# Hybrid decoder block on one core: other places in the SBUF partition for the matmul operands

## The chip, the cores and the metric

One NeuronCore of a Trainium2 chip runs the whole program. The metric is the device time of one execution in microseconds (us); a run's number is that of the core. "Span" is the time from the first to the last instruction in a profiled execution.

## The reference

One decoder block on x of shape (1, 256, 2048) in float32, with a conditioning vector c:

```
mod = silu(c) @ w_ada + b_ada                      # six vectors of 2048: sh1, sc1, gt1, sh2, sc2, gt2
h = rms_norm(x, norm1_gain) * (1 + sc1) + sh1
p = h @ w_in + b_in                                # 2048 -> 8736 columns
y_rwkv = rwkv7_branch(p[...])                      # 16 heads of 64, a scan over the 256 tokens
y_attn = sliding_window_sink_attention(p[...])     # 16 heads of 64, window 128
merged = sig(g_rwkv) * (y_rwkv @ w_branch_rwkv) + sig(g_attn) * (y_attn @ w_branch_attn)
x = x + gt1 * (merged @ w_out)
h = rms_norm(x, norm2_gain) * (1 + sc2) + sh2
x = x + gt2 * (square(relu(h @ w_up)) @ w_down)    # 2048 -> 8192 -> 2048
return rms_norm(x, final_gain)
```

## The kernel before

**Matmuls in two halves.** Every big product runs in float32r with both operands split: a value is the sum of a rounded part "hi" and a rest "lo", and three of the four products are kept (hi·hi, hi·lo, lo·hi). A piece of 512 KB of weights is loaded into a tile `raw` (L286, L325, queue of SP); ScalarE casts it into `whi` (L274) and VectorE subtracts to get `wlo` (L275). There are 7 `raw`, 4 `whi` and 4 `wlo` buffers of 4096 bytes a partition. Every matmul record in the trace has a weight load (LDWEIGHTS, "PEld") of its stationary operand beside it.

**Two forms of product.** `feed` (L278) has the weights stationary (128 columns, 512 bytes a partition) and activations as the moving rows (256 tokens, 1024 bytes). One piece of weights makes 24 such matmuls:

```
for wt, xs in ((hi, (xh, xl)), (lo, (xh,))):            # L291
    for kk in range(n):
        ...
            for xx in xs:
                TE.matmul(ps[...], lhsT=wt[:, kk, o:o + m], rhs=xx(k), ...)   # L297
```

`rows_product` (L309) has it the other way round: 128 tokens of the activations are stationary and 512 columns of a weight part move (L319).

**Order of the work.** The four parts of the input product (L948 to L984, pieces of w_in over 4 blocks of k each, 384 matmuls in a part) come first, with the vectors sc1 and sh1 of the next part made beside them on VectorE by `ada_dve` (L207). Then come gates, keys and the attention branch's product with `a1` and `a2` as moving rows (L1006 to L1034), while the RWKV chain, attention and further `ada` vectors are put between the pieces by `pulse` (L253), in an order that is fixed when the program is built. Then: the RWKV branch's product with two `tt` tiles as moving rows (L1039), the output product (L1095, stationary rows `m`), the first three column products of the up matrix from rows not yet normalised (`zhi`, `zlo`, 258 columns, 96 matmuls in each product, L1111 to L1140), and the MLP in 8 groups: `up(g + 1)` (4 column products of 96 matmuls, rows `h2`), then `down(g)` (192 matmuls of 512 columns, stationary rows `u`, L1181). `ada_vec(5)` runs beside the MLP; its sums are small matmuls (L186) between the pieces.

**Places in the partition.** Pools stand one behind the other: `const`, `wp` (`raw`, `acc`, `whi`, `wlo`), `hp` (the four tiles of 8192 bytes that hold `h`, then `m`, then `h2`), and `mx`, which is closed after the branch products and whose room the pool `ml` takes. The address of a tile is the sum of the sizes before it, each rounded up to 32 bytes. Tag `ug` has three slots, each as long as its longest tile, 16512 bytes for `zlo`. From the sizes, in bytes from the start of the partition, and the rest by 512:

| tile | role in the matmul | place before | rest by 512 |
|---|---|---|---|
| whi, wlo | weights' parts | 56384 + 4096 i | 64 |
| h, m, h2 (hp) | moving, stationary, moving | 89152 + 8192 i | 64 |
| tt (two) | moving | 146496, 154688 | 64 |
| a1, a2 | moving | 186880, 195072 | 0 |
| zhi, zlo | moving, rows of 1032 bytes | 187840, 171328 | 448, 320 |
| u, slot 1 (groups 1, 4, 7) | stationary | 138304 | 64 |
| u, slot 2 (groups 0, 3, 6) | stationary | 154816 | 192 |
| u, slot 3 (groups 2, 5) | stationary | 171328 | 320 |

"Offset" below is the moving row's place less the stationary row's, as a rest by 512. Before the change it is 0 for `h`, `h2`, `tt` and `m`, 448 for `a1` and `a2`, and 0, 384 and 256 for `u` in slots 1, 2 and 3.

Of the kernel before, what the change touches and what calls it, by code (L numbers as in the profile page):

```python
# [10 lines left out]
F32 = mybir.dt.float32  # L11
F32R = mybir.dt.float32r
# [6 lines left out]
P = 128  # L19
T = 256  # L20
D = 2048
KC = D // P
# [16 lines left out]
RATE_BG = (0.9, 0.3, 0.4, 0.2)  # L39
RATE_Z = 2.0  # L40
NCH = T // L
NORM_EPS = 1e-6
GN_EPS = 64e-5
KAPPA = -math.exp(-0.5)
# [9 lines left out]
def _constants():  # L54
# [19 lines left out]
    k[:, K_DI + P:K_DI + 2 * P] = np.where((dp >= 0) & (dp < WIN), dp, far)  # L74
    rs = np.ones((NCH, L + 1), np.float32)
    rs[:, 0] = 0
    k[:, K_RS:K_RS + NCH * (L + 1)] = rs.reshape(1, -1)
    k[:, K_ON:K_ON + P] = 1.0
# [4 lines left out]
def hybrid_block(ctx: ExitStack, tc, x, c, w_ada, b_ada, norm1_gain, w_in, b_in, rwkv_mix, rwkv_w0,  # L83
# [4 lines left out]
    V, S, G, TE = nc.vector, nc.scalar, nc.gpsimd, nc.tensor  # L88

    const = ctx.enter_context(tc.tile_pool(name="const", bufs=1))  # L90
    wp = ctx.enter_context(tc.tile_pool(name="wp", bufs=2))
    hp = ctx.enter_context(tc.tile_pool(name="hp", bufs=1))
    mm = ctx.enter_context(tc.tile_pool(name="mm", bufs=NMM, space=PSUM))
    ax = ctx.enter_context(tc.tile_pool(name="ax", bufs=8 - NMM, space=PSUM))

# [9 lines left out]
    def ps_ax():  # L105
        return ax.tile([P, 512], F32, tag="ax", name=nm("ax"))
# [25 lines left out]
    mx = mx_ctx.enter_context(tc.tile_pool(name="mx", bufs=1, reuse_waits="tile"))  # L132

    def tl(tag, shape=(T,), bufs=1, dt=F32):
        return mx.tile([P] + list(shape), dt, tag=tag, bufs=bufs, name=nm(tag))
# [167 lines left out]
    def cols_product(w, kblocks, c0, widths, xh, xl):  # L303
        ps = ps_mm()
        for k0 in range(0, kblocks, 8):
            feed(w, k0, 8, [(c0, sum(widths))], [(ps, j, m) for j, m in enumerate(widths)], xh, xl, 0, kblocks - 1)
        return ps
# [61 lines left out]
    def rstd_of(dst, ss, n, eps, t):  # L369
        V.tensor_scalar(ss, ss, 1.0 / n, eps, op0=ALU.mult, op1=ALU.add)  # L370
        rsqrt(dst, ss, t)
# [20 lines left out]
    for tb in range(2):  # L392
        S.activation(sq, xt[tb][:], AF.Square, accum_out=st_s[:, tb:tb + 1])
    rstd_of(st_s[:, 2:4], st_s[:, 0:2], D, NORM_EPS, st_s[:, 4:6])
    for _ in range(2):
# [3 lines left out]
    for k2 in range(KC // 2):  # L399
        ps = ps_ax()  # L400
# [50 lines left out]
    def c4(t):  # L451
        return t.rearrange("p (c t) -> p c t", c=NCH)

# [26 lines left out]
    def prep(ss, st):  # L480
# [3 lines left out]
        g4 = st["g4"][:, j]  # L484
        st["ar"] = ar = tl("ar", (2, NCH, 2, L), 2)
        st["tok"] = tok = {n: tl(n, (2, NCH, L), 2) for n in ("vt", "bt", "kt")}
        st["bv"] = bv = tl("bv", (2, T), 2)
        for i in range(2):
            b = 2 * ss + i
            kT, rT, vT = [st["in"][:, n, i, :] for n in range(3)]  # L490
            p4 = tl("p4", (4 * T + NCH,), 2)
            aT, eN, kk = [p4[:, o * T:(o + 1) * T] for o in range(3)]
# [304 lines left out]


    W3 = 3 * P
    vtok = mx.tile([P, 2, P], F32, name="vtok")  # L800
    yad = tc.dram_tile([8, P, T], F32, name="yad")

    arena = [tl("a1", (8 * T,)), tl("a2", (8 * T,))]
# [1 line left out]
    def slot(a, o, n, shape):  # L805
        return arena[a][:, o:o + n].rearrange("p (a b) -> p a b", a=shape)
# [64 lines left out]
    def pair(q2, qT=None):  # L871
        if qT is None:
            qT = qas[q2 % 2]
            nc.sync.dma_start(qT.rearrange("p a b -> p (a b)"), qd[q2])
        yield from zipped([attention(2 * q2 + i, qT[:, i]) for i in range(2)])
# [19 lines left out]
    def begin_attention():  # L895
        kvf = slot(0, 0, 2 * T, 2)
        for i in range(2):
            S.activation(kvf[:, i, :], e_kv[:, i * T:(i + 1) * T], AF.Identity,
                         bias=colA[:, A_BK + i:A_BK + i + 1], scale=1.0)
        q0 = qas[0]  # L900
        for i in range(2):
            S.activation(q0[:, i, :], e_q[:, i * T:(i + 1) * T], AF.Identity, bias=q8[:, i:i + 1], scale=0.125)
        for kv in range(2):
            for hh in range(2):
                G.tensor_copy(kd[HS[hh], kv, :], kvf[HS[kv], 0, :])
        ps = ps_ax()
        for kb in range(2):
            TE.transpose(ps[:, kb * P:(kb + 1) * P], kvf[:, 1, kb * P:(kb + 1) * P], ident)
        S.copy(vtok[:].rearrange("p a b -> p (a b)"), ps[:, 0:2 * P])
        for q2 in range(4):  # L910
            att.append(pair(q2, q0 if q2 == 0 else None))

# [35 lines left out]
    for part, nk in enumerate(SL):  # L948
# [9 lines left out]
        for g2 in range(0, len(sums), 2):  # L958
            two = sums[g2:g2 + 2]
            ps = [ps_ax() for _ in two]  # L960
            feed(w_in, k0, nk, [(c, 256) for _, c in two], [(p, j, P) for p in ps for j in range(2)],
                 hA, hB, k0, k0 + nk - 1)
            for a, ((what, n), _) in enumerate(two):
                t, j = rest[g2 + a]
                o = flat(t, j)
                if part == 0:
                    S.copy(o, ps[a][:])
                else:
                    V.tensor_tensor(o, ps[a][:], o, op=ALU.add)  # L969
                if last:  # L970
                    t = t[:, 2 * j:2 * j + 2, :]
                    if what == "g":
                        gate_out(n, t, o)
                    elif what == "q":
                        for j in range(2):
                            S.activation(t[:, j, :], t[:, j, :], AF.Identity, bias=q8[:, 2 * n + j:2 * n + j + 1],
                                         scale=0.125)
                        nc.sync.dma_start(qd[n], o)
            if last and g2 == 2:
                finish(bg)  # L980
                begin_heads()
                begin_attention()
                rate["rw"], rate["att"] = RATE_RW, RATE_ATT
# [43 lines left out]
    for g in range(8):  # L1027
# [4 lines left out]
        ps = cols_product(w_branch_attn, 8, g * 256, [P, P], yh, yl)  # L1032
# [6 lines left out]
    for g in range(8):  # L1039
# [4 lines left out]
        ps = cols_product(w_branch_rwkv, 8, g * 256, [P, P], yh, yl)  # L1044
# [8 lines left out]


    ml = ctx.enter_context(tc.tile_pool(name="ml", bufs=1, reuse_waits="tile"))
    x1 = ml.tile([P, 2, D], F32, name="x1")
    for tb in range(2):
        nc.sync.dma_start(x1[:, tb, :], x[tb * P:(tb + 1) * P, :])
# [1 line left out]

    TW = T + 2
    zhi = ml.tile([P, KC, TW], F32R, tag="acc", name="zhi")
    zlo = ml.tile([P, KC, TW], F32R, tag="ug", bufs=3, name="zlo")
    wide = ml.tile([P, KC, P], F32, tag="fg", name="wide1")
    gt1 = ml.tile([P, D], F32, tag="gt", name="gt1")

    V.tensor_scalar(gtc[:, 0:KC], gtc[:, 0:KC], 0.5, None, op0=ALU.mult)
    ss2 = ml.tile([P, 16], F32, name="ss2")

    def scaled(ks):  # L1070
        for k in ks:
# [5 lines left out]
    def turned(cg):  # L1077
        for k in (cg * 4, cg * 4 + 2):
            ps = ps_ax()
            for i in range(2):  # L1080
                for tb in range(2):
                    TE.transpose(ps[:, i * T + tb * P:i * T + (tb + 1) * P],
                                 x1[:, tb, (k + i) * P:(k + i + 1) * P], ident)
            S.copy(x1T[:, k:k + 2, :].rearrange("p a b -> p (a b)"), ps[:])
# [27 lines left out]
    V.tensor_reduce(ss2[:, 8:10], ss2[:, 0:8].rearrange("p (a b) -> p a b", a=2), axis=AX.X, op=ALU.add)  # L1112
    rstd_of(ss2[:, 10:12], ss2[:, 8:10], D, NORM_EPS, ss2[:, 14:16])
    turned(3)
# [5 lines left out]
    ps = ps_ax()  # L1120
# [51 lines left out]
    def down(g, u):  # L1172
        for cg in range(4):
# [9 lines left out]
            for tb in range(2):  # L1183
# [5 lines left out]
                else:  # L1189
# [6 lines left out]
                    if cg == 2:  # L1196
                        h = ss2[:, 8 + tb:9 + tb]
                        V.tensor_reduce(h, ss2[:, 4 * tb:4 * tb + 3], axis=AX.X, op=ALU.add)
                        V.tensor_scalar(h, h, 0.5 / D, 0.5 * NORM_EPS, op0=ALU.mult, op1=ALU.add)
                    if cg == 3:  # L1200
# [61 lines left out]
```

## Time and profile before

| | us |
|---|---|
| median of 3 runs | 1566.24 (1565.78 to 1566.56) |
| the profiled execution's own time | 1566.93 |
| its span | 1565.1 |
| PE (matmuls) busy in the span | 1510.9 |
| PEld (weight loads) busy | 1385.8 |
| VectorE (DVE) busy | 1100.7 |
| ScalarE (ACT) busy | 722.6 |
| mean granted TensorE clock | 0.987 of full |

Busy time of PE says that a matmul was under way, not at what pace. Matmuls overlap: one of 256 columns lasts some 280 ns in the record, while the next starts 113 to 120 ns later. So the pace has to be read from the starts, or from a stretch of the chain of work with its count of matmuls ("x384" in 46.07 us is 120.0 ns each).

### The profile page before, as it was taken

The numbers are of one execution on the slowest core, as the hardware profiler recorded it, in microseconds if no ns is written. First come the engines' busy times: TensorE is split into PE (matmuls) and PEld (weight loads), VectorE is DVE, ScalarE is ACT, GpSimd is POOL, SyncE is SP. The second block draws the span as 40 slices with busy tenths as digits, with TensorE's granted clock in tenths as the row PEclk, the third lists the DMA queues.
The fourth block names the chain that finished last, engine by engine and source line by source line (L and its number), as shares of the span: only waits on it lengthen the run. The fifth ranks groups of instructions, "written<-read, shape, count | busy, mean of one in ns | idle before, by whom it ended". The sixth has DMA issues, their size and how long they took to land.

```text
span 1565.1 us, 30120 instructions
## 1 busy us (share of the span) xinstructions
PE 1510.9 (97%) x12122; PEld 1385.8 (89%) x12122; DVE 1100.7 (70%) x1784; ACT 722.6 (46%) x1107; POOL 40.5 (3%) x97
## 2 busy tenths in 40 slices
PE   5899999999999999999999999999999999999997
PEld 2898999889989898989889998989898898989985
DVE  1879979867789857669769755666666666555576
ACT  3353377655355433345447444434444343444443
POOL 2000000030000030000000000000000000000000
PEclk9899999999999999999999999999999999999999
DMA  9999978869888859849865777677776776566652
GB/s 343 335 325 295 342 234 245 245 170 310 283 262 285 269 155 297 282 147 339 285 215 173 240 222 228 216 222 226 225 228 211 227 222 205 184 188 189 194 183 81
DMA packets 297100, 372.80 MB, mean 238 GB/s; under 512 B 40912, under 2 KB 198384, under 8 KB 296320
## 3 DMA queue, kind: packets, MB, share of 16 engines
q1 hardware_dynamic: 296448, 370.72, 74.7%
q8 instruction: 95, 1.56, 0.4%
q0 software_dynamic: 512, 0.15, 0.1%
q14 instruction: 45, 0.37, 0.1%
HBM read 357.96 MB, written 12.86 MB: 237 GB/s over the span
## 4 chain that ended last, share of the span: by engine, by line
PE 87%; DVE 4%; DMA 3%; ACT 2%; issue 2%; POOL 1%; SPq 0%; POOLq 0%; DVEq 0%; ACTq 0%
PE mm L297 41%; PE mm L319 14%; PE ax L319 14%; PE ax L297 9%; PE ax L683 2%; PE ax L186 1%; PE ax L478 1%; DVE wlo L275 1%; DVE acc L219 1%; PE ax L566 1%; DMA ada<-in_w_ada_dram 1%; ACT whi L274 1%; DMA tt<-in_x_dram 1%; PE ax L653 0%; PE ax L237 0%
## 5 line engine op out<-in xcount | busy, mean ns | idle before, releaser
L274 ACT CAST whi<-raw 128x1024 fp32r<-128x1024 f32 x458 | 478.0, 1047 | 673.4 <-PE mm L297 257.0
L275 DVE TENSOR_TENSOR wlo<-raw,whi 128x1024 fp32r<-128x1024 f32 x458 | 557.0, 1219 | 267.3 <-ACT whi L274 258.6
L297 PE MATMUL mm<-h,whi 128*128 128x256 f32 (+1 forms) x3296 | 446.8, 286 | 3.4 <-ACT whi L274 3.4
L297 PEld LDWEIGHTS mm<-h,whi 128*128 128x128 f32 (+1 forms) x3296 | 415.2, 192 | 10.1 <-ACT whi L274 3.4
L219 DVE SCALAR_TENSOR_TENSOR acc<-ada,cact,acc 128x512 f32<-128x512 f32 x330 | 247.0, 749 | 60.2 <-DMA ada<-in_w_ada_dram 55.6
L297 PE MATMUL mm<-h,wlo 128*128 128x256 f32 (+1 forms) x1648 | 237.7, 284 | 0.0
L297 PEld LDWEIGHTS mm<-h,wlo 128*128 128x128 f32 (+1 forms) x1648 | 215.0, 191 | 1.1 <-issue 0.7
L319 PE MATMUL mm<-whi,u 128*128 128x512 f32 x512 | 138.3, 392 | 0.0
L319 PE MATMUL ax<-whi,u 128*128 128x512 f32 x512 | 138.0, 391 | 0.0
L297 PE MATMUL ax<-h,whi 128*128 128x256 f32 x768 | 109.0, 290 | 9.0 <-DVE p L969 4.5
L319 PEld LDWEIGHTS ax<-whi,u 128*128 128x128 f32 x512 | 96.2, 188 | 21.0
L319 PEld LDWEIGHTS mm<-whi,u 128*128 128x128 f32 x512 | 95.6, 188 | 20.2
L297 PEld LDWEIGHTS ax<-h,whi 128*128 128x128 f32 x768 | 100.2, 197 | 11.4 <-ACT whi L274 5.0
L319 PE MATMUL ax<-wlo,u 128*128 128x512 f32 x256 | 79.4, 391 | 0.0
L319 PE MATMUL mm<-wlo,u 128*128 128x512 f32 x256 | 79.3, 391 | 0.0
L297 PE MATMUL ax<-h,wlo 128*128 128x256 f32 x384 | 59.2, 287 | 0.0
L319 PEld LDWEIGHTS mm<-wlo,u 128*128 128x128 f32 x256 | 48.1, 188 | 10.5
L319 PEld LDWEIGHTS ax<-wlo,u 128*128 128x128 f32 x256 | 48.1, 188 | 10.5
L297 PEld LDWEIGHTS ax<-h,wlo 128*128 128x128 f32 x384 | 52.6, 197 | 0.1
L297 PE MATMUL mm<-tt,whi 128*128 128x256 f32 x256 | 37.7, 298 | 2.1 <-ACT tt L768 2.1
L297 PEld LDWEIGHTS mm<-tt,whi 128*128 128x128 f32 x256 | 34.5, 203 | 3.2 <-ACT tt L768 2.3
L319 PE MATMUL mm<-whi,m 128*128 128x512 f32 x128 | 35.0, 392 | 0.0
(345 smaller groups left out, 1489.1 us busy)
## 6 DMA issues: line engine op xcount, KB each, us to landing
ada<-in_w_ada_dram SPq DMA_DIRECT2D x192, 512.0 KB, 5.5
raw<-in_w_up_dram SPq DMA_DIRECT2D x128, 512.0 KB, 3.9
raw<-in_w_down_dram SPq DMA_DIRECT2D x128, 512.0 KB, 4.0
raw<-in_w_in_dram SPq DMA_DIRECT2D x72, 512.0 KB, 5.2
raw<-in_w_in_dram SPq DMA_DIRECT2D x128, 256.0 KB, 5.1
raw<-in_w_out_dram SPq DMA_DIRECT2D x32, 512.0 KB, 6.1
raw<-in_w_branch_attn_dram SPq DMA_DIRECT2D x16, 512.0 KB, 5.9
raw<-in_w_branch_rwkv_dram SPq DMA_DIRECT2D x16, 512.0 KB, 5.2
```

The costliest lines, as they stand in the source:

```text
L186: TE.matmul(ps[:, j:j + 1], lhsT=acc[:, j * P:(j + 1) * P], rhs=ones[:, 0:1], start=True, stop=True)
L219: V.scalar_tensor_tensor(o, in0=t[:, a, :], scalar=ck, in1=o, op0=ALU.mult, op1=ALU.add)
L274: S.copy(hi[:], raw[:])
L275: V.tensor_tensor(lo[:], raw[:], hi[:].bitcast(F32), op=ALU.subtract)
L297: TE.matmul(ps[0:m, j * tw:(j + 1) * tw], lhsT=wt[:, kk, o:o + m], rhs=xx(k), start=(k == begin and xx is xh and wt is hi and j == 0), sto ...
L319: TE.matmul(pss[tb][:], lhsT=uu(k)[:, sl], rhs=wt[:, kk, :], start=(first and k == 0), stop=(final and k == kblocks - 1))
L478: TE.matmul(out[hs, :], lhsT=src[hs, chunk(c)], rhs=ident[hs, hs], start=True, stop=True)
L566: TE.matmul(pT[hs, o:o + P], lhsT=src[hs, chunk(c)], rhs=ar[hs, i, c].rearrange("p a b -> p (a b)"), start=True, stop=True)
L683: TE.matmul(ps[hs, j, i, part, :], lhsT=lhs(j, i, hs), rhs=rhs(j, i, hs), start=(first and j == 0 and i == 0), stop=True, skip_group_check ...
```

## The change

No instruction is added, removed or reordered. A tile of 448 bytes that nobody uses stands ahead of `hp`'s tiles; `vtok` gets 64 bytes behind it; `zlo` gets 384 bytes behind it, so that a slot of `ug` is 16896 bytes, a multiple of 512; `ss2` (64 bytes) is allocated ahead of `x1` instead of behind `gt1`.

```diff
+PAD_H, PAD_A, PAD_Z = 112, 16, 96
     hp = ctx.enter_context(tc.tile_pool(name="hp", bufs=1))
+    hp.tile([P, PAD_H], F32, name="pad_h")
...
-    vtok = mx.tile([P, 2, P], F32, name="vtok")
+    vtok = mx.tile([P, 2 * P + PAD_A], F32, name="vtok")[:, 0:2 * P].rearrange("p (a b) -> p a b", a=2)
...
-        S.copy(vtok[:].rearrange("p a b -> p (a b)"), ps[:, 0:2 * P])
+        S.copy(vtok.rearrange("p a b -> p (a b)"), ps[:, 0:2 * P])
...
     ml = ctx.enter_context(tc.tile_pool(name="ml", bufs=1, reuse_waits="tile"))
+    ss2 = ml.tile([P, 16], F32, name="ss2")
...
-    zlo = ml.tile([P, KC, TW], F32R, tag="ug", bufs=3, name="zlo")
+    zlo = ml.tile([P, KC * TW + PAD_Z], F32R, tag="ug", bufs=3, name="zlo")[:, 0:KC * TW] \
+        .rearrange("p (a b) -> p a b", b=TW)
...
-    ss2 = ml.tile([P, 16], F32, name="ss2")
```

By the same sums the places become: `h`, `m`, `h2` 89600 + 8192 i (rest 0), `tt` 146944 and 155136 (rest 0), `a1` and `a2` 187392 and 195584 (rest 0, as before), `zhi` 189504 and `zlo` 172608 (rest 64), `u` 138816, 155712 and 172608 (rest 64). `whi` and `wlo` stay. So the offset becomes 448 for `h`, `h2` and `tt`, stays 448 for `a1` and `a2`, becomes 64 for `m`, and 0 for `u` in all three slots.

## Rows read from the trace of the kernel before

**Rows 1.** The page: busy time and share of each engine; the chain by engine.
```profile
PE 1510.9 (97%) x12122; PEld 1385.8 (89%) x12122; DVE 1100.7 (70%) x1784; ACT 722.6 (46%) x1107; POOL 40.5 (3%) x97
...
PE 87%; DVE 4%; DMA 3%; ACT 2%; issue 2%; POOL 1%; SPq 0%; POOLq 0%; DVEq 0%; ACTq 0%
```

**Rows 2.** Stretches by stage: length, busy time (instructions) by engine, clock, DMA share, GB/s.
```profile
40.00:209.00 169.00, 158.03 (x1250) 155.47 (x1251) 147.21 (x195) 70.05 (x89) 0.00 (x0) 0.96 0.97 321
209.00:266.00 57.00, 56.23 (x476) 53.89 (x476) 47.89 (x114) 47.85 (x112) 1.80 (x6) 1.00 0.78 235
266.00:664.00 398.00, 387.02 (x4634) 362.77 (x4631) 305.58 (x644) 185.91 (x375) 29.08 (x68) 0.99 0.82 255
664.00:730.00 66.00, 63.85 (x519) 58.96 (x515) 50.91 (x143) 32.88 (x61) 0.00 (x0) 0.95 0.67 214
730.00:820.00 90.00, 89.97 (x434) 75.23 (x434) 67.41 (x96) 43.54 (x66) 0.00 (x0) 1.00 0.80 275
...
861.00:1556.00 695.00, 693.54 (x4391) 630.32 (x4389) 432.31 (x475) 296.04 (x331) 0.00 (x0) 1.00 0.66 205
```

**Rows 3.** Groups by line and shape, PE: count, busy us, mean ns, idle before.
```profile
L297 PE MATMUL mm<-h,whi 128*128 128x256 f32 x3264 | 442.8, 286 | 3.4 <-ACT whi L274 3.4
L297 PE MATMUL mm<-h,wlo 128*128 128x256 f32 x1632 | 235.5, 284 | 0.0
...
L297 PE MATMUL ax<-h,whi 128*128 128x256 f32 x768 | 109.0, 290 | 9.0 <-DVE p L969 4.5 <-ACT whi L274 3.7 <-DVE rn L518 0.7
...
L297 PE MATMUL ax<-h,wlo 128*128 128x256 f32 x384 | 59.2, 287 | 0.0
L297 PE MATMUL mm<-tt,whi 128*128 128x256 f32 x256 | 37.7, 298 | 2.1 <-ACT tt L768 2.1
...
L297 PE MATMUL mm<-tt,wlo 128*128 128x256 f32 x128 | 19.2, 294 | 0.0
```

**Rows 4.** Chain of waits, late stages: start us, us, instructions merged.
```profile
731.16 0.91 PE ax L319 x4
...
850.22 11.56 PE ax L297 x96
...
899.93 19.44 PE mm L297 x162
...
963.99 25.91 PE mm L297 x216
990.69 20.26 PE mm L297 x168
1054.49 46.07 PE mm L297 x384
```

**Rows 5.** Timeline of PE, attention branch's product: start us, us, matmuls merged.
```profile
480.08 2.05 PE L297 MATMUL mm<-a,whi 128*128 128x256 f32 x16
...
530.19 1.98 PE L297 MATMUL mm<-a,whi 128*128 128x256 f32 x16
532.01 1.07 PE L297 MATMUL mm<-a,wlo 128*128 128x256 f32 x8
532.91 0.75 PE L297 MATMUL mm<-h,whi 128*128 128x256 f32 x5
...
579.31 1.98 PE L297 MATMUL mm<-a,whi 128*128 128x256 f32 x16
...
611.73 2.05 PE L297 MATMUL mm<-a,whi 128*128 128x256 f32 x16
```

**Rows 6.** Chain of waits, second part of the input product.
```profile
124.15 0.74 DVE acc L219
...
133.37 5.06 PE ax L297 x40
```

**Rows 7.** Stretches after a wait of the RWKV chain, columns as in rows 2.
```profile
588.00:592.00 4.00, 1.99 (x32) 1.80 (x32) 3.53 (x6) 0.00 (x0) 0.00 (x0) 0.60 0.92 200
592.00:596.00 4.00, 3.74 (x40) 3.62 (x41) 0.69 (x1) 0.56 (x1) 0.00 (x0) 0.55 1.01 291
```

## The prediction

> **What bounds the kernel now.** I read the page first: PE is busy for 97% of the span and is 87% of the chain that ended last [rows 1]. Then the stretches by stage. From 861 us on, PE is idle for 1.5 of 695 us, with VectorE at 62% and DMA at 0.66; from 266 to 664 us it is idle for 11 of 398 us; only from 40 to 209 us is it idle for 11 of 169 us, with VectorE busy for 87% and DMA at 0.97 [rows 2]. So the kernel is bound by the pace at which matmuls follow each other, and the change, which touches no instruction, can act only on that pace. The rest is to find the pace at each offset.
>
> **The pace at offset 0.** An up product is 384 matmuls in 46.07 us, 120.0 ns each [rows 4]; rows `h2` against the weights' parts, offset 0.
>
> **The pace at offset 448.** The kernel before already holds one product with this offset: the attention branch's, with `a1` and `a2`, of the same shape and from the same weight buffers. Its 24 matmuls from 530.19 to 532.91 us take 2.72 us, 113.3 ns each [rows 5]. It does not always settle there. Of its 11 stretches of at least 19 matmuls with no other between, eight settle so (sixteen matmuls in 1.98 us); three, the first at 480.08 and the last at 611.73 us, have 2.05 us for the same sixteen [rows 5], which over 15 starts is 4.7 ns more, 118.0 ns. A stretch keeps its pace to its end. Two of these three begin right behind the small sums of L186. So offset 448 saves 6.7 ns a matmul at the pace of 113, 2.0 at that of 118, and by eight to three 5.4 on average.
>
> **Down product.** Group 0 (slot 2, offset 384) lies between the end of one stretch, 899.93 + 19.44 = 919.37, and 963.99 us: 44.62 us for 192 matmuls, 232.4 ns. Group 1 (slot 1, offset 0) lies between 990.69 + 20.26 = 1010.95 and 1054.49 us: 43.54 us, 226.8 ns [rows 4]. The change gives all groups offset 0.
>
> **The change part by part.** There are 3264 + 1632 + 768 + 384 = 6048 matmuls with `h` or `h2` and 384 with `tt` that go from offset 0 to 448 [rows 3]. By stage:
> - Up products: 29 column products of 96, 2784 matmuls, on the path entirely. Stretches that follow L186 (168 matmuls from 990.69 us, and 360 in a later group) I put at 118: 528 × 2.0 = 1.1 us. The other 2256 at 113: 2256 × 6.7 = 15.1 us. Sum 16.2 us; ends 2784 × 2.0 = 5.6 and 2784 × 6.7 = 18.7.
> - RWKV branch: 384 × 5.4 = 2.1 us, less a little for waits on the chain's rows (PE is idle for 2.2 of 66 us [rows 2]): 2.0.
> - From 266 to 664 us: 18 column products of 96, 1728 × 5.4 = 9.3 us. What now hides behind PE there is the RWKV chain's own latency and VectorE at 77%; PE order is fixed, so some waits grow. With 3% idle now I take three quarters, 7.0 us; ends 0 and 1728 × 6.7 = 11.6.
> - Input product: four parts of 384. The last part has no `ada` vectors beside it and PE at 99% [rows 2]: 384 × 5.4 = 2.1 us. In the others VectorE is the chain from 124.15 to 133.37 us, and all of it from the part's start keeps VectorE near full; what comes behind, 133.4 to 157.6 us, is PE [rows 6]: 24.2 us is some 200 matmuls, 1.1 us a part, 3.4 in three. What PE saves ahead of 124 us only lengthens its wait for VectorE. Sum 5.5; ends 2.1 and 1536 × 6.7 = 10.3.
> - Down product: 1.08 us for each of groups 0, 3 and 6, 3.3 us in all.
> - Output product: 384 matmuls of 512 columns, now 4 in 0.91 us [rows 4], go from offset 0 to 64. No row has offset 64. Below, the saving of offset 448: 384 × 6.7 = 2.6 us; above, the loss of offset 384: 384 × 5.6 = 2.2 us. For 512 columns two of three offsets give 226.8 and one is worse, so I take 0.
> - Rows `zhi` and `zlo`: 288 matmuls of 258 columns whose offset moves by 8 bytes with each k. Now 96 take 11.56 us, 120.4 ns, spread over offsets 256 to 504 [rows 4]; after, 0 to 120. I take 0; ends 288 × 7 = 2.0 us gained (113.3) and 288 × 3 = 0.9 lost (the 2.5% of the down groups).
> - All else that moves (small matmuls of RWKV and attention, ScalarE and VectorE operands): 0, with 1.5 us either way, 2.5% of some 60 us of small matmuls on the path.
> - Room that is used again: `x1T` now ends 64 bytes inside the second `tt` tile. Its first write comes behind the output product's first quarter, and the `tt` rows were last read by the branch product before it; no wait is new. No queue changes order.
>
> The gains add up to 16.2 + 2.0 + 7.0 + 5.5 + 3.3 = 34.0 us. The profiled execution took 1566.9 us, 0.7 above the median of the runs, so 1532.9 by its own time and 1532.2 by the median; I say **1533**.
>
> **A page that speaks against it.** The trace has 113.3 against 120.0 ns, and 226.8 against 232.4, for matmuls that differ in nothing I can find but place [rows 4, 5]. The Trainium skill ("TensorE: Matmul & The Clock Gate", Part 2, step-by-step) says that PE reads moving rows and weights through two independent ports, so that loading the next weights takes no read bandwidth from the running matmul. By that rule the places are indifferent and the time stays at 1566; the two pairs of rows say otherwise, so it gets the chance of the third rival below and no more.
>
> **The rivals.**
> 1. *The long up stretches settle at 118 ns.* They all begin behind a matmul of 512 columns, which no stretch of `a1` does, and since they are alike they may all go one way. For it: three of eleven. Against: eight of eleven, and two of the three stand behind L186. Up products then give 5.6 instead of 16.2: 1533 + 10.6 = 1544.
> 2. *Other work eats what is saved before 664 us.* VectorE, DMA and the RWKV chain's latency take the place of PE, and 7.0 + 5.5 are lost: 1533 + 12.5 = 1545. Against it: PE has 97% there from 266 us on.
> 3. *Place is not the cause,* and `a1` differs for some other reason (what lies between, other data): the time stays at 1566. Against it: the 24 matmuls at 530 us are `a` alone, in the same loop and the same buffers as `h`, and slot 2 of `u` differs from slot 1 in place alone.
> 4. *The clock.* Where PE waits for the chain the granted clock falls: from 588 to 596 us, behind a wait in which PE was busy for about half, it was 0.60 and 0.55, near 1.2 GHz, a loss of 8 × 0.42 = 3.4 us [rows 7]. If faster matmuls uncover more such waits from 40 to 664 us, the gains there vanish (rival 2) and each wait costs 3.4 us more. The remaining 21.5 us are used up by six to seven; ten would make 1566 + 34 - 21.5 = 1579, slower. Against it: VectorE and DMA have room from 209 to 664 us, and the saved time is 2% of that stretch.
>
> **How the numbers follow.** Forecast 0.65; rival 1 0.17; rival 2 0.08; rival 3 0.05; rival 4 0.03; 0.02 for larger gains than the range holds. Low end: 113 ns everywhere and most of the early gains, 18.7 + 2.5 + 9.5 + 7.5 + 3.3 = 41.5, with about half of what `m` and `zhi` could give besides: 1522. High end: rivals 1 and 2, partly together, 34.0 - 10.6 - 10 = 13.4 us of gain: 1553. A measurement of this kernel tells about 0.2%, 3 us, from no change. Faster: 0.65 + 0.17 + 0.08 + 0.02 = 0.92; same: 0.05; slower: 0.03.
>
> **What would show it.** In the profile after: up stretches "x384" of 43.5 us (113.3 ns) if right, 45.3 for rival 1, 46.07 for rival 3; groups of the down product 43.5 us each, also 0, 3 and 6; the input product's second part ending about 1 us sooner after its start, with a longer VectorE piece in its chain; from 266 to 664 us the stretch shorter by 7 us with little more idle time of PE; the output product's 0.91 us for 4 unchanged. The forecast is wrong if `h` at offset 448 doesn't settle at the pace of `a1`, or if the clock's mean falls clearly below 0.987.

## The result and the profile after

The changed kernel takes 1550.0 us in the median of 4 runs (1544.0 to 1553.3), against 1566.4 (1565.8 to 1566.8) before: ratio 0.9894, interval 0.9871 to 0.9918. So it is faster, by 16.4 us, about half of the 33 that were forecast and inside the stated range. In a later set of runs, on which the experiments below were measured, it took 1553.0 us (6 runs) against 1564.7 (17 runs, 1559.4 to 1570.6): 0.9922, interval 0.9894 to 0.9950. The profiled execution took 1546.8 us, with a span of 1545.0; the sums below are made against that one, which is 20.1 us shorter in its span than the one before.

In the page after, the busy times of PE and the chain by engine (as in [rows 1]):

```profile
PE 1487.1 (96%) x12122; PEld 1363.7 (88%) x12122; DVE 1099.5 (71%) x1784; ACT 723.6 (47%) x1107; POOL 40.2 (3%) x97
...
PE 82%; DMA 6%; DVE 5%; issue 2%; POOL 2%; ACT 2%; SPq 1%; POOLq 0%; DVEq 0%; ACTq 0%
```

The instructions are as many as before; PE's busy time fell by 23.8 us, the span by 20.1. The new lines sit four lines lower in the file: L297 is now L301, L319 is L323, L186 is L190.

The chain of waits in the late stages, after (start, length, merged instructions; as in [rows 4]):

```profile
951.08 25.44 PE mm L301 x216
977.30 19.89 PE mm L301 x168
1040.74 45.23 PE mm L301 x384
1130.44 45.23 PE mm L301 x384
```

An up stretch of 384 takes 45.23 us, 117.8 ns a matmul, and every one of them does. The stretches of 168 and 360 behind L190 stand at 117.8 ns as well, once they are under way. The forecast had 43.5 us (113.3 ns) for 384; 45.3 was what rival 1 named. Group 0 of the down product now ends its 192 matmuls within 43.6 us (907.51 to 951.08), as group 1 does: 226.9 ns each, the pace of offset 0.

The earlier stages, before, cut at the first matmul of each (length, busy time by engine, clock, DMA share, GB/s):

```profile
41.20:255.70 214.50, 203.98 (x1623) 200.17 (x1624) 184.94 (x282) 109.76 (x184) 1.80 (x6) 0.97 0.92 298
255.70:477.20 221.50, 216.65 (x2542) 199.63 (x2540) 173.77 (x400) 120.93 (x272) 14.94 (x35) 1.00 0.83 257
477.20:669.90 192.70, 184.42 (x2234) 175.77 (x2233) 143.71 (x271) 73.85 (x123) 14.14 (x33) 0.97 0.82 257
669.90:730.10 60.20, 60.17 (x473) 55.61 (x474) 48.08 (x139) 31.05 (x57) 0.00 (x0) 0.94 0.64 208
```

And after (input product; gates, keys and attention; attention branch and RWKV chain; RWKV branch):

```profile
40.10:249.90 209.80, 198.23 (x1625) 193.99 (x1625) 185.83 (x286) 110.60 (x185) 1.79 (x6) 0.97 0.94 308
249.90:471.60 221.70, 213.96 (x2541) 196.97 (x2538) 172.85 (x397) 120.53 (x271) 14.71 (x35) 0.99 0.82 254
471.60:660.60 189.00, 181.05 (x2235) 172.38 (x2234) 143.50 (x272) 74.09 (x123) 14.05 (x33) 0.98 0.84 262
660.60:718.40 57.80, 57.75 (x473) 53.07 (x474) 47.27 (x138) 31.10 (x57) 0.00 (x0) 0.97 0.67 218
```

The second of these stages did not get shorter, though its matmuls with `h` follow each other faster: PE is idle for 7.7 us in it where it was for 4.9, and the mean clock fell from 1.00 to 0.99.

The terms of the forecast against the profiled execution, each the difference between the times from one stage's first matmul to the next stage's:

| term | forecast, us gained | measured |
|---|---|---|
| input product (with 1.1 us at its start) | 5.5 | 5.9 |
| 266 to 664 us | 7.0 | 3.5 |
| RWKV branch | 2.0 | 2.3 |
| output product (`m`) | 0 | -1.1 |
| `zhi`, `zlo` | 0 | 0.2 |
| up products | 16.2 | 6.0 |
| down product | 3.3 | 3.3 |
| sum | 34.0 | 20.1 |

Two of these are near the forecast for another reason. Of the 5.9 us, 1.1 lie before the first matmul with `h`, where the place of `h` cannot count. Of the 2.3 us in the RWKV branch, 1.7 are one fall of the clock fewer: the mean clock there was 0.94 over 60.2 us and is 0.97 over 57.8. The pace itself gave 0.6 us, because the long stretch of 284 with `tt` stands at 117.8 ns.

### The profile page after: what moved, and what is told of

It is laid out like the page before. It is cut to its first block, busy times and chain, and to the rows that moved or that the text cites. A ratio compares the mean times of both kernels' runs of the same rounds, so it can differ in the third digit from the quotient of the medians.

```text
span 1545.0 us, 30120 instructions
## 1 busy us (share of the span) xinstructions
PE 1487.1 (96%) x12122; PEld 1363.7 (88%) x12122; DVE 1099.5 (71%) x1784; ACT 723.6 (47%) x1107; POOL 40.2 (3%) x97
## 4 chain that ended last, share of the span: by engine, by line
PE 82%; DMA 6%; DVE 5%; issue 2%; POOL 2%; ACT 2%; SPq 1%; POOLq 0%; DVEq 0%; ACTq 0%
PE mm L301 37%; PE mm L323 14%; PE ax L323 14%; PE ax L301 8%; DMA raw<-in_w_in_dram 2%; PE ax L687 1%; DVE wlo L279 1%; DMA ada<-in_w_ada_dram 1%; DVE acc L223 1%; PE ax L482 1%; PE ax L190 1%; PE ax L570 1%; POOL p L625 1%; POOL rs L623 1%; DMA scr<-p 1%
## 5 line engine op out<-in xcount | busy, mean ns | idle before, releaser
L301 PE MATMUL mm<-h,whi 128*128 128x256 f32 (+1 forms) x3296 | 437.2, 283 | 3.4 <-ACT whi L278 3.4
L301 PEld LDWEIGHTS mm<-h,whi 128*128 128x128 f32 (+1 forms) x3296 | 405.4, 189 | 10.6 <-ACT whi L278 3.4
L301 PE MATMUL mm<-h,wlo 128*128 128x256 f32 (+1 forms) x1648 | 232.3, 281 | 0.0
L301 PEld LDWEIGHTS mm<-h,wlo 128*128 128x128 f32 (+1 forms) x1648 | 209.8, 188 | 1.0 <-issue 0.7
L323 PE MATMUL mm<-whi,u 128*128 128x512 f32 x512 | 137.2, 390 | 0.0
L323 PE MATMUL ax<-whi,u 128*128 128x512 f32 x512 | 136.9, 389 | 0.0
L301 PE MATMUL ax<-h,whi 128*128 128x256 f32 x768 | 105.6, 286 | 10.0 <-DVE p L973 4.9
L323 PEld LDWEIGHTS ax<-whi,u 128*128 128x128 f32 x512 | 96.1, 188 | 20.0
L323 PEld LDWEIGHTS mm<-whi,u 128*128 128x128 f32 x512 | 95.5, 188 | 19.3
L301 PEld LDWEIGHTS ax<-h,whi 128*128 128x128 f32 x768 | 96.9, 193 | 12.5 <-ACT whi L278 6.2
L323 PE MATMUL mm<-wlo,u 128*128 128x512 f32 x256 | 78.8, 389 | 0.0
L323 PE MATMUL ax<-wlo,u 128*128 128x512 f32 x256 | 78.8, 389 | 0.0
L301 PE MATMUL ax<-h,wlo 128*128 128x256 f32 x384 | 57.9, 284 | 0.0
L323 PEld LDWEIGHTS mm<-wlo,u 128*128 128x128 f32 x256 | 48.1, 188 | 10.0
L323 PEld LDWEIGHTS ax<-wlo,u 128*128 128x128 f32 x256 | 48.1, 188 | 10.0
L301 PEld LDWEIGHTS ax<-h,wlo 128*128 128x128 f32 x384 | 51.5, 195 | 0.0
L301 PE MATMUL mm<-tt,whi 128*128 128x256 f32 x256 | 35.9, 289 | 2.2 <-ACT tt L772 2.2
L301 PEld LDWEIGHTS mm<-tt,whi 128*128 128x128 f32 x256 | 32.8, 195 | 3.2 <-ACT tt L772 2.3
L323 PE MATMUL mm<-whi,m 128*128 128x512 f32 x128 | 35.4, 395 | 0.0
```

Source lines behind the costliest of these rows:

```text
L301: TE.matmul(ps[0:m, j * tw:(j + 1) * tw], lhsT=wt[:, kk, o:o + m], rhs=xx(k), start=(k == begin and xx is xh and wt is hi and j == 0), sto ...
L323: TE.matmul(pss[tb][:], lhsT=uu(k)[:, sl], rhs=wt[:, kk, :], start=(first and k == 0), stop=(final and k == kblocks - 1))
```

## The experiments

The question was why the up stretches stand at 117.8 ns where the attention branch's rows with the same offset mostly reached 113.3. Theory: offset 448 allows both paces, and what precedes a stretch decides which. Rivals: `h2` cannot reach 113.3 at all, or it is chance.

**Only the tiles of `hp` moved.**

```diff
--- before
+    hp.tile([P, 112], F32, name="pad_h")
...
+    hq = ctx.enter_context(tc.tile_pool(name="hq", bufs=1))
+    hq.tile([P, 16], F32, name="pad_q")
```

> Only h, m and h2 move (offset 448 for h and h2, 64 for m); tt, u, zhi and zlo keep their rests by 512. Theory (an up stretch behind a 512-column matmul settles at 117.8 ns, 2.2 ns under offset 0): up stretches of 384 in 45.2 us, some 6 us of gain in the up products, some 9 us up to the branch product as in the changed kernel, m at about 230 ns (1 us lost), tt at 120.0 and down groups 0, 3 and 6 at 232 as before: about 1552 us. Rival (the 117.8 comes from the new place of u or zhi ahead of the stretch, not from h2's own offset): up stretches at 113.3 ns or 120.0 ns, about 1540 or 1558 us.

It took 1548.8 us (6 runs, 1542.4 to 1554.9), ratio 0.9894, interval 0.9867 to 0.9921. The chain of waits of this kernel, late stages:

```profile
854.37 54.41 PE mm L300 x480
...
953.40 24.49 PE mm L300 x216
978.67 19.89 PE mm L300 x168
1042.11 45.23 PE mm L300 x384
...
1222.55 43.53 PE mm L300 x384
...
1313.23 42.51 PE mm L300 x360
```

Neither theory nor rival had this: the same product in the same loop, with the same rows, takes 43.53 us in one stretch and 45.23 in others. Three stretches are at 113.3 ns here. Two are those behind groups 0 and 3 of the down product, whose `u` stands at offset 384 in this kernel (slot 2, as before the change); behind slots 1 and 3, and behind L190 (here L189), it is 117.8. The third is the first and longest, 480 matmuls in 54.41 us, behind the rows `zhi` and `zlo`, which keep their rests by 512 in this kernel; in the changed kernel these rows have moved, and the same 480 take 56.53 us. So `h2` can reach 113.3, and the pace goes with the place of the rows ahead. From the first matmul with `h2` to the end this kernel takes 692.6 us, the changed one 694.2, though its down groups 0, 3 and 6 are still at 232 ns: moving `u`, and with it `zhi` and `zlo`, gave 3.3 us in the down product and took away the start at 113.3 of three long stretches, 4.8 us.

**Only `u` (with `zlo`, `zhi`) moved.**

```diff
--- before
-    zlo = ml.tile([P, KC, TW], F32R, tag="ug", bufs=3, name="zlo")
+    zlo = ml.tile([P, KC * TW + 96], F32R, tag="ug", bufs=3, name="zlo")[:, 0:KC * TW] \
+        .rearrange("p (a b) -> p a b", b=TW)
```

> Only the slots of u (and zlo, zhi) move, u to offset 0 in all groups. Theory: 576 matmuls from 232 to 227 ns, 3.2 us less, 1563 us, and up stretches stay at 120.0 ns. Rival (the pace of the down product hangs on something else in groups 0, 3 and 6): no change, 1566 us.

It took 1564.0 us (12 runs), ratio 0.9999 with an interval of 0.9979 to 1.0019, which cannot tell 3 us from none: the runs of the kernel before beside it spread over 11 us. The trace can. Chain of waits of this kernel:

```profile
899.92 22.32 PE mm L297 x186
...
965.79 25.91 PE mm L297 x216
```

Group 0 lies between 922.24 and 965.79 us: 43.55 us, where it was 44.62. From the first matmul with `h2` to the end it is 700.4 us against 703.5 before, the 3.1 us expected, and up stretches stay at 120.0 ns (25.91 us for 216).

**Small matmuls ahead of the up stretches.** In the profile after, between 250 and 735 us, 14 of 16 stretches at full clock of at least 19 matmuls with `h` that begin behind 64x64 matmuls of the RWKV chain settle at 113.3 ns, two at 117.8; in the other profiles at offset 448 it is 12 of 16 up to all. So a pair of 64x64 matmuls was put ahead:

```diff
--- after
+    def nudge():
+        ps = ps_ax()
+        for h in range(2):
+            hs = slice(h * L, (h + 1) * L)
+            TE.matmul(ps[hs, 0:L], lhsT=ident[hs, hs], rhs=ident[hs, hs], start=True, stop=True)
...
         ada_sum(acc, n, dst, k0, seg, gain)
+        if seg == 5:
+            nudge()
...
+                if c2 == (NZ if g == 0 else 0):
+                    nudge()
                 ps = cols_product(w_up, KC, g * 1024 + c2 * 256, [P, P], hA, hB)
```

> The changed kernel with two small 64x64 matmuls put in front of each up stretch and behind each L186 sum of the last ada vector (12 such pairs, their result is not used). Theory (the pace is settled at the start of a stretch by the matmul ahead of it; behind 64x64 matmuls stretches of h settled at 113.3 ns nearly always): up stretches of 384 in 43.5 us, 2784 x 4.5 ns = 12.4 us less, for some 4 us of cost (0.35 us for each pair and refill): about 8 us under the changed kernel. Rival (h2's rows or this stage cannot settle at 113.3): up stretches stay at 117.8 ns and the time is 4 us over the changed kernel's.

Timeline of PE in this kernel at the start of an up stretch, then the chain of waits:

```profile
1134.13 0.33 PE L237 MATMUL ax<-kt 64*64 64x64 f32 x4
1134.39 2.10 PE L309 MATMUL mm<-h,whi 128*128 128x256 f32 x16
```

```profile
982.56 19.26 PE mm L309 x168
1045.62 43.74 PE mm L309 x384
1134.46 43.74 PE mm L309 x384
...
1314.83 41.02 PE mm L309 x360
```

Every up stretch, those behind L190 too, is at 113.3 ns; 43.74 is 43.5 with a restart of 0.2 us. It took 1543.8 us (5 runs, 1538.7 to 1546.4), ratio 0.9858, interval 0.9833 to 0.9884, 9.2 us under the changed kernel on the same chip. From the first matmul with `h2` to the end it is 686.8 us against 694.2: 12.4 us saved, less 12 pairs at some 0.4 us. So in the late stage what stands ahead of a stretch sets its pace, and the stretch keeps it. An interruption alone is not enough: the sums of L190 interrupt PE as well, and in the late stage of the changed kernel the stretches behind them stay at 117.8. Which property of the pair counts (its shape, the place of its rows) was not tried.

**The changed kernel again.**

> The changed kernel itself. Theory: its runs spread over some 9 us because stretches ahead of 730 us settle now at 113.3, now at 117.8 ns, by how the waits fall in that execution; up stretches are at 117.8 in each execution. A profile of 1553 us would show more of the early stretches at 117.8 or a lower clock in one stage, and none in the up products. Rival: the up stretches differ from execution to execution.

1553.0 us in 6 runs. The chain of waits of this execution:

```profile
955.68 25.44 PE mm L301 x216
...
1045.34 45.23 PE mm L301 x384
...
1403.15 45.23 PE mm L301 x384
```

The up stretches agree to 0.01 us with those of the first profile, and from the first matmul with `h2` to the end both take 694.2 us. Its span is 4.6 us longer all the same, and all of that, and a little more, lies in the earlier stages: up to the first matmul with `tt` this execution gained 3.2 us on the one before, the first profile 9.4. Of these 6.2 us, 2.1 lie before the first matmul with `h`, and 3.4 are lost to two more falls of the clock behind the input product, each 3.4 us long at half of full speed. Paces change there too: the 284 matmuls with `tt` behind the same sums of L190 stand at 117.8 ns in the first profile and at 113.3 in this one. So ahead of the late stage the matmul ahead does not fix the pace alone; in the late stage nothing changed between the two.

**All of `u` at offset 384.**

```diff
--- after
-PAD_H, PAD_A, PAD_Z = 112, 16, 96
+PAD_H, PAD_A, PAD_Z, PAD_S = 112, 16, 96, 48
...
-    ss2 = ml.tile([P, 16], F32, name="ss2")
+    ss2 = ml.tile([P, PAD_S], F32, name="ss2")[:, 0:16]
```

> The changed kernel with all three slots of u at offset 384 instead of 0 (ss2's tile 128 bytes longer). Theory (the matmul ahead settles a stretch; behind rows of u at 384 the first run on e1 settled at 113.3, behind u at 0 and 256 at 117.8): every up stretch behind a down group at 113.3 ns, 43.5 us for 384, and every down group at 232 ns, 44.6 us; the stretches behind L190 stay at 117.8. From the first h2 matmul to the end 693 us, against 694.2. Rival (which stretches settle at 113.3 is chance): some at 113.3, some at 117.8.

```profile
852.95 54.40 PE mm L301 x480
...
1130.95 43.53 PE mm L301 x384
1219.98 45.23 PE mm L301 x384
...
1313.33 42.51 PE mm L301 x360
1400.64 43.52 PE mm L301 x384
```

In the chain of waits above, five of six stretches behind the down groups are at 113.3 ns; one, at 1219.98 us, is at 117.8, and so are those behind L190. The 480 behind `zhi` and `zlo`, which stand at another rest here too, are at 113.3. So rows at offset 384 ahead favour the lower pace but do not force it: in the late stage the theory holds for the small matmuls and only mostly here. One down group lasts from 1085.46 to 1130.95 us, 45.5 us with a sum of L190 in it. The late stage took 694.8 us, no better than the change, since what the up stretches gained the slower down groups lost; in one run the kernel took 1549.3 us.

**Other offsets of `h`, `h2`, `tt`, `a1` and `a2`.** These kernels differ from the changed one only in the two pads (PAD_H, and ss2's length, so that `u` stays at offset 0). For offset 64:

```diff
--- after
-PAD_H, PAD_A, PAD_Z = 112, 16, 96
+PAD_H, PAD_A, PAD_Z, PAD_S = 16, 16, 96, 112
...
-    ss2 = ml.tile([P, 16], F32, name="ss2")
+    ss2 = ml.tile([P, PAD_S], F32, name="ss2")[:, 0:16]
```

PAD_H and PAD_S are 32 and 96 for offset 128, 64 and 64 for 256, 80 and 48 for 320, 96 and 32 for 384, 120 and 136 for 480.

> The changed kernel with h, h2, tt, a1 and a2 64 bytes past the weights' parts (offset 64 in place of 448), and m's weights 448 past m's rows; u stays at offset 0. Theory: each offset has its own set of paces to settle at, read from the up stretches of 384: 46.1 us (120.0 ns), 45.2 (117.8) or 43.5 (113.3); at 64 no guess better than 45.2. m: 227 ns if 448 is the better side for 512 columns too, against 230 to 231 in the changed kernel. Rival (only whether the offset is 0 matters): 45.2 us at every offset but 0.

> As s64 with offset 128 (m: 384). Theory: an own pace; m at 232 ns, as u had at 384. Rival: up stretches of 384 in 45.2 us as at 448, and m at 230 to 231.

> As s64 with offset 256 (m: 256). Theory: an own pace; m at 227 ns, as u had at 256. Rival: up stretches of 384 in 45.2 us as at 448.

> The changed kernel with h, h2, tt, a1 and a2 at offset 320 (m: 192). Theory (the pace goes by the distance of the two places on a ring of 512 bytes: 120.0 at 0 and 256, 118.7 to 120.0 at 128 and 384): as at 64 or 448, 117.8 with some 113.3, if the ring repeats after 256 bytes. Rival (only next to 0 is better): 118.7 to 120.0.

> As s64 with offset 384 (m: 128). Theory: an own pace; rows zhi and zlo at spread offsets suggest none much over 120 ns. Rival: up stretches of 384 in 45.2 us as at 448.

> The changed kernel with h, h2, tt, a1 and a2 at offset 480 (m: 32). Theory: between 448 (117.8 or 113.3) and 0 (120.0): no pace under 113.3; 113.3 in every stretch if 448 is past the best place. Rival: 120.0 as at offset 0, if places count in steps of 64 bytes.

One row of the chain of waits of each, an up stretch of 384, in this order of offsets: 64, 128, 256, 320, 384, 480.

```profile
1134.50 45.23 PE mm L301 x384
```

```profile
1139.60 46.08 PE mm L301 x384
```

```profile
1143.27 46.07 PE mm L301 x384
```

```profile
1133.87 45.23 PE mm L301 x384
```

```profile
1138.12 46.08 PE mm L301 x384
```

```profile
1144.26 45.44 PE mm L301 x384
```

And the last stretch with `tt` of the kernel with offset 320, behind L190:

```profile
688.52 32.30 PE mm L301 x284
```

| offset of `h2` | pace behind a down group, ns | behind L190, ns | one run, us |
|---|---|---|---|
| 0 (before) | 120.0 | 120.0 | 1566.9 |
| 64 | 117.8 | 117.8 | 1551.0 |
| 128 | 120.0 | 118.7 | 1558.9 |
| 256 | 120.0 | 120.0 | 1563.1 |
| 320 | 117.8 | 117.8 | 1550.3 |
| 384 | 120.0 | 118.7 | 1557.5 |
| 448 (the change) | 117.8, with other rows ahead 113.3 | 117.8, with a pair ahead 113.3 | 1546.8 |
| 480 | 118.3 | 118.3 | 1561.6 |

Each offset has its own paces. The rival that only 0 is bad falls: 256 is as bad as 0, and 384 as bad as 128. 64 and 320 also give the same, so the pace seems to repeat after 256 bytes; 192, the partner of 448, was not tried. 480 is not better than 448. Of all that were tried, 448 alone shows 113.3 in an up stretch. The lower pace is not 448's alone, though: at 320 the 284 matmuls with `tt` take 32.30 us, 113.7 ns each, where at 64 they stand at 117.8.

The rows `m` moved in these kernels too, and the first 96 matmuls of the output product tell the pace of 512 columns at each place. At offsets 0 and 256 they start 227 ns apart, at 128 and 384 232.3, at 32, 192 and 448 233.3 to 233.4, and at 64 (the change) 233.4 in the first profile and 228.9 in the second. So 448 is not the better side for 512 columns, as had been thought possible ahead of the run with 64; the 232 and 227 ns expected at 384 and 256 came.

One rival stands untested. The weights' parts stood at rest 64 in every kernel, and in each kind of product one operand alone was moved. So these runs do not tell whether the distance between the two operands counts, or the place of the moved one by itself.

**Fewer pairs.** From the small matmuls those are left out that no long stretch follows, and two are added behind L190 ahead of stretches of 216 and 284.

```diff
--- small matmuls ahead of the up stretches
-        if seg == 5:
+        if (seg, k0) in ((4, 8), (3, 4), (5, 0), (5, 12)):
...
-                if c2 == (NZ if g == 0 else 0):
+                if c2 == (NZ if g == 0 else 0) and g != 1:
```

> As e3, with pairs of small matmuls only where a long stretch follows: ahead of the 7 up stretches, and behind 4 sums of L190 (ahead of stretches of 216, 284, 168 and 360). Theory: up stretches at 113.3, 12.4 us less than the changed kernel for 9 x 0.41 us; the stretches of 216 and 284 at 113.3, 2.2 us less for 0.8: about 10 us under the changed kernel, 1541 us. Rival (the clock takes it back ahead of 730 us): 1546 us or more, with more falls of the clock than e3's ten.

```profile
852.90 54.62 PE mm L309 x480
...
1217.08 43.74 PE mm L309 x384
```

In its chain of waits all up stretches are at 113.3 ns, and the late stage takes 685.6 us. Of the two pairs that were added, one did what was expected: the 216 behind it, rows `a1`, `a2` and `h`, are at 113.3 ns. The other missed: the 284 with `tt` settle at 117.8, behind a pair that ran while the clock was at half. So a pair does not always bring the lower pace. It took 1540.7 us (4 runs, 1538.7 to 1545.0), ratio 0.9856 to the kernel before, interval 0.9833 to 0.9879: the best of the kernels run, and not to be told apart from the one with 12 pairs.

**What comes ahead of 664 us.** The stage of gates, keys and attention, up to the first matmul with `a1`, in the profiles at hand. `h` at offset 0, only `u` moved:

```profile
255.10:477.50 222.40, 217.09 (x2542) 199.88 (x2540) 173.92 (x400) 120.88 (x272) 14.84 (x35) 1.00 0.81 255
```

`h` at 448: only `hp` moved, then the changed kernel again, then the one with 12 pairs:

```profile
246.40:471.50 225.10, 217.48 (x2541) 199.40 (x2539) 173.74 (x400) 121.08 (x272) 14.86 (x35) 0.98 0.80 252
```

```profile
253.00:476.20 223.20, 215.01 (x2542) 198.18 (x2540) 172.75 (x397) 120.78 (x271) 14.91 (x35) 0.98 0.81 252
```

```profile
251.50:478.20 226.70, 219.85 (x2542) 201.02 (x2540) 172.84 (x397) 120.54 (x271) 14.91 (x35) 0.96 0.79 248
```

At offset 0 the mean clock is 1.00 and PE idle for 5 us; at 448 the clock is 0.96 to 0.99 and PE idle for 7 to 8. A clock of 0.96 over 227 us is 9 us lost, one of 0.98 over 224 us 4.5. Where it falls can be seen in the attention's softmax, before:

```profile
338.00:342.00 4.00, 1.90 (x20) 1.69 (x19) 3.86 (x4) 4.00 (x8) 3.69 (x5) 1.00 0.00 0
342.00:346.00 4.00, 3.94 (x38) 3.39 (x35) 1.42 (x3) 2.73 (x8) 3.21 (x11) 1.00 0.02 4
```

and after:

```profile
332.00:336.00 4.00, 1.47 (x12) 1.28 (x12) 3.88 (x4) 4.00 (x8) 3.69 (x5) 0.93 0.00 0
336.00:340.00 4.00, 4.00 (x30) 3.54 (x28) 0.89 (x2) 2.32 (x7) 3.23 (x11) 0.65 0.01 4
```

PE waits here for ScalarE's copy of the transposed softmax (L857, now L861) for 2.1 us before and 2.5 after: its own matmuls are done sooner and ScalarE is not. Behind the longer wait the granted clock falls to half, 1.2 GHz, for 3.4 us (0.93 and 0.65 of two stretches of 4 us), which it does not behind the shorter one. The length of the wait does not decide it, though. With only `hp` moved the same wait was longer still, and no fall followed:

```profile
332.83 0.43 PE L865 MATMUL ax<-a,vtok 128*64 128x128 f32 x2 [2.80 <-ACT a L860]
...
336.00:340.00 4.00, 4.00 (x36) 3.83 (x34) 1.71 (x2) 1.64 (x3) 1.46 (x5) 1.00 0.47 57
```

In the kernel with 12 pairs it was shorter (the longest wait in the first line), and one followed:

```profile
PE ax L874 <- ACT a L869: 4.7, 3, 2.3
...
340.00:344.00 4.00, 4.00 (x24) 3.46 (x23) 0.88 (x2) 2.26 (x6) 3.08 (x13) 0.59 0.02 4
```

Over the whole stage the two kernels at offset 0 have no fall of the clock, and each of the six profiles at 448 has 3.4 to 17 us at half. That goes with more idle time of PE, but what sets off a single fall stays open. This was read from traces, not tried: no run took the wait away.

## Why the prediction was right or wrong

- *That place sets which paces a matmul can have, and both paces of offset 448, 113.3 and 118 ns* (read from the attention branch's rows): right to 0.2 ns. Rival 3 is refuted by the offset runs. The Trainium skill ("TensorE: Matmul & The Clock Gate", Part 2, step-by-step) states that loading weights takes no read bandwidth from a running matmul; as far as that is read to mean that places are indifferent, these runs speak against it, with 113.3 to 120.0 ns for the same matmul.
- *Up products, 16.2 us:* the step that failed, worth 10.2 us. "The other 2256 at 113" took a share of eight to three from stretches that begin behind other matmuls than these do. All stretches behind the 512-column matmuls of `u` at offset 0 settle at 117.8, and so do the first 480 behind `zhi` and `zlo`: 6.0 us. That is rival 1, which had the right time for this stage (5.6 us) and half of the reason: what stands ahead counts, but a matmul of 512 columns ahead does not by itself bring 117.8, as those of `u` at offset 384 show. A chance of 0.17 was too small for what no row had shown. The 528 behind L190 were right at 117.8.
- *From 266 to 664 us, 7.0 us:* too large, the second step that failed. In the profile after it is 3.5. Over the six profiles at offset 448 (the changed kernel twice, only `hp` moved, all of `u` at 384, and both kernels with pairs) the two stages last 410.1 to 415.8 us, mean 413.3, against 414.2 and 417.9 at offset 0 (before, and only `u` moved), mean 416.0: some 2.7 us, less than these profiles differ among themselves. Taken apart (PE's idle time, then half of the time at the lower clock as lost to the clock, then the rest), the pace gave about 6.9 us of the 9.3 that the forecast began with; idle time took back 1.7 and the clock 2.6. So rival 4's mechanism is at work here: waits of PE grow from 5 to 7 or 8 us in the first of the two stages, and the clock falls more often. It was priced at 3.4 us a fall, where those that came on top mostly cost 1.7 and some 5.1, and called improbable because VectorE and DMA have room; the wait of PE that grew in the softmax is one for ScalarE.
- *Input product 5.5, RWKV branch 2.0, down product 3.3:* 5.9, 2.3 and 3.3 in the profile. The down product was right. The other two are right in size and in part by luck: 1.1 us of the first lie before any matmul with `h`, and 1.7 of the second are the clock, so that the pace gave 4.8 and 0.6.
- *Output product, 0 between 2.6 gained and 2.2 lost:* 1.1 lost. Offset 64 costs 512-column matmuls about 3 ns, as the upper bound from offset 384 allowed.
- *`zhi` and `zlo`, and all else that moves, 0:* 0.2 us.
- *The sum:* 34 forecast; 20 in the profile and 16 in the median, inside the range of 1522 to 1553 because rival 1, which came true, and part of what rivals 2 and 4 describe had been let in.

## What to carry to other kernels

Where PE is bound by its own pace, look at the distance between moving and stationary operands in the partition: here 448 bytes instead of 0, by a rest of 512, is worth 2 to 7 ns in 120 for 256 columns, and 0 or 256 instead of 384 worth 6 in 232 for 512 columns. A stretch of like matmuls keeps the pace at which it starts, so read which matmul stands ahead of each long stretch; a pair of small ones cost 0.4 us and gave 1.7 us in each up stretch of 384. What a faster stretch saves beside engines that are not faster shows in part as idle time and as a lower clock, so take such a stage apart into pace, idle time and clock. And where a pace taken from a sister product comes in two values, forecast the two cases apart by what precedes, not by their share.

## What the runs showed of the hardware

- Matmuls of 256 columns settle at one of a few fixed paces, 113.3, 117.8, 118.3, 118.7 or 120.0 ns, by the offset of the two operands. Offsets 448 and 320 show both 113.3 and 117.8; at 448, which of the two goes with what ran just before. A stretch keeps its pace for up to 480 matmuls. That the distance counts, and not the place of the moved rows alone, is not shown.
- At 512 columns the places count the other way round: offset 0 and 256 give 226.8 ns, 128 and 384 232, 448 233, while 0 and 256 are the worst for 256 columns (120.0).
- With the faster pace PE waited more in the stage of gates, keys and attention, and its clock stood at 1.2 GHz for 3.4 to 17 us there, in six profiles, where it never did in the two at offset 0; a wait's length alone did not tell (2.80 us without a fall, 2.3 with one). The runs of the kernel before spread over 1559 to 1571 us in the second set, more than the 0.2% on which the forecast had counted.
